# A hybrid attention layer on one core: the first value weights loaded before the second tile of x and rounded on another engine, and one of four partial products left out of the value product

## The chip, the cores and the metric

The kernel runs on one core of a Trainium2 chip. The metric is the time of one execution in microseconds (us); the median of three runs is given. The engines are named as in the profile: PE is TensorE's matmuls, PEld its weight loads, DVE is VectorE, ACT ScalarE, POOL GpSimd, and SP is SyncE, which issues all loads and stores of this kernel in one queue. Names like L365 are line numbers of the kernel before; behind line 494 the changed file's numbers are one lower.

## The reference

One layer on x of 1024 rows by 1024 columns, in float32. Only the first part is touched by the change:

```python
h = rmsnorm(x, norm_mix_g)
z = h @ w_in        # [qA|kA|vA|qB|kB|vB|gA|gB]
# differential attention: 4 heads, two score maps a head, values of width 128
sc = einsum('bqhcd,bkhcd->bchqk', rope(qA), rope(kA)) * 64 ** -0.5
sc = where(k_chunk <= q_chunk, sc, -1e30)      # chunks of 64 rows
p = softmax(sc)
attn = p[:, 0] - lam * p[:, 1]
o = einsum('bhqk,bkhd->bqhd', attn, vA)        # the value product
yA = rmsnorm(o, subln_g) * (1 - lam_init)
# then: band attention yB (8 heads), gated merge, cross attention to 256
# memory rows, a SwiGLU block of inner width 2816, final rmsnorm
```

## The kernel before

**Two parts for each number.** Every float32 operand of a large product is split in two numbers of TensorE's faster fp32r type: `hi`, the operand rounded, and `lo`, the remainder `src - hi` (`split`, L72 to L79). The rounding is a copy on ScalarE (L74) or an operation on GpSimd (L78), as the argument `hi_eng` says; the remainder is taken on VectorE (L79). A product of two split operands then takes three matmuls into one bank, hi by hi, lo by hi and hi by lo (`prod`, L89, and `prod_steps`, L212).

**The value product is built otherwise.** For a block of 128 queries and a block of 128 keys, the transposed probabilities `pt` (hi and lo) are the stationary operands, and the moving one is 256 columns of `v`: 128 columns of v's hi beside 128 columns of v's lo. L364 multiplies pt's hi and L365 pt's lo with all 256, into the bank `av`; that makes four products, hi and lo of `pt` with hi and lo of `v`. At the end of a block the two halves of the bank are added (L369 and L370). A head has 8 query blocks with 1 to 8 key blocks, 36 pairs, and each pair has one L364 and one L365.

**Weights.** `unit` (L81) issues the load of 128 x 1024 weights into `raw` (2 buffers) and splits it into `wsp` (3 buffers). `Units` holds the weights of one job; `Feed` is the list of projection jobs, which the attention code steps through between its own matmuls, so that TensorE has projections (L215 to L217, bank `acc`, two of these) to do while the softmax runs on other engines. `v_jobs(g, ..)` makes the 8 jobs that project one group of values, with two weight units a group; group 0 is the first work of the feed.

**The start.** The loop at L489 goes over 8 tiles of x of 128 rows: load the tile, (for the first) load the gain, then `norm_T`: mean square on ScalarE (L106), reciprocal root on GpSimd (L99, L101), scaling on VectorE (L108), and 8 transposes on TensorE (L120), four into the bank `tr` and four into the bank `av`. Each bank is split by ScalarE (L74) and VectorE (L79) into the stationary tiles `t`. There is one `tr` bank and one `av` bank, so a tile's transposes wait until the banks of the tile before are split. Behind the second tile the first value weights are loaded, and then the value projections follow the tiles at a distance of one.

**The differential attention.** A `UnitA` is one head and one block of 128 queries. `s` makes the scores in a bank `s` (L310, L311; two of these), VectorE takes the maximum (L333), ScalarE the exponentials (L334), and VectorE the difference of the two maps (L340). `tr` transposes up to four key blocks of the result into the one bank `tr` (L350) and splits it into `pt`; `avs` is the value product; `end`, two steps later, transposes the finished block, again in the bank `tr` (L382), and ScalarE copies it out into `yt` (L383). The next transposes of probabilities (L350) can't begin before that copy has emptied the bank.

**The order of the instructions** on each engine is not that of the code: a scheduler reorders the program when it is built, and each engine then works through its row in order.

Of the kernel before, what the change touches and what calls it, by code (L numbers as in the profile page):

```python
# [15 lines left out]
P = 128  # L16
# [19 lines left out]
def build(tc, x, mem, wqk, wv, wg, wup, wout, wcq, wck, wcv, wco, wgu, wdn,  # L36
          bias, lamv, subln_g, g_mix, g_cross, g_mem, g_ffn, g_final, rope, out):
    nc = tc.nc
    pe, act, dve, pool, sp = nc.tensor, nc.scalar, nc.vector, nc.gpsimd, nc.sync
# [17 lines left out]
    def acc_tile():  # L57
        return psum.tile([P, HALF], F32, name="acc", tag="acc", bufs=2)
# [7 lines left out]
    def av_tile():  # L66
        return psum.tile([P, HALF], F32, name="av", tag="av", bufs=1)
# [4 lines left out]
    def split(hi, lo, src, hi_eng, lo_eng):  # L72
        if hi_eng is act:
            act.copy(out=hi, in_=src)  # L74
        elif hi_eng is dve:
            dve.tensor_copy(out=hi, in_=src)
        else:
            pool.tensor_scalar(out=hi, in0=src, scalar1=1.0, scalar2=0.0, op0=ALU.mult, op1=ALU.add)  # L78
        lo_eng.tensor_tensor(out=lo, in0=src, in1=hi.bitcast(F32), op=ALU.subtract)  # L79

    def unit(src, hi_eng=act):  # L81

        raw = wp.tile([P, D], F32, name="raw", tag="raw", bufs=2)
        sp.dma_start(out=raw, in_=src)
        w = wp.tile([P, 2, D], F32R, name="wsp", tag="wsp", bufs=3)
        split(w[:, 0], w[:, 1], raw, hi_eng, dve)
        return w
# [9 lines left out]
    def rstd_of(ss, n):  # L97
        ms = sm.tile([P, 1], F32, name="ms")
        pool.tensor_scalar(out=ms, in0=ss, scalar1=1.0 / n, scalar2=EPS, op0=ALU.mult, op1=ALU.add)  # L99
        r = sm.tile([P, 1], F32, name="rstd")  # L100
        pool.tensor_tensor(out=r, in0=ms, in1=mhalf, op=ALU.pow)  # L101
        return r

    def rms(xt, gbc, dst):
        ss = sm.tile([P, 1], F32, name="ss")
        act.activation(dst, xt, AF.Square, accum_out=ss)  # L106
        r = rstd_of(ss, D)
        dve.scalar_tensor_tensor(out=dst, in0=xt, scalar=r, in1=gbc, op0=ALU.mult, op1=ALU.mult)  # L108

    def norm_T(xt, gbc, xn, dst_of):  # L110

        rms(xt, gbc, xn)
        to_T(xn, dst_of)

    def to_T(xn, dst_of):
        for g in range(2):
            ps = (tr_tile if g == 0 else av_tile)()
            for i in range(4):
                k = g * 4 + i
                pe.transpose(out=ps[:, i * P:(i + 1) * P], in_=xn[:, k * P:(k + 1) * P], identity=ident)  # L120
            hi, lo = dst_of(g)
            v = ps.rearrange("p (a b) -> p a b", a=4)
            split(hi, lo, v, act, dve)
# [88 lines left out]
    def prod_steps(acc, terms, us):  # L212
        n = len(terms)
        for i, (lh, ll, rh, rl) in enumerate(terms):
            pe.matmul(acc, lh, rh, start=(i == 0), stop=False)  # L215
            pe.matmul(acc, ll, rh, start=False, stop=False)  # L216
            pe.matmul(acc, lh, rl, start=False, stop=(i == n - 1))  # L217
            yield us
# [9 lines left out]
    with tc.tile_pool(name="at", bufs=1, reuse_waits="tile") as at:  # L228
        stage[:] = [lambda: at.tile([P, HALF], F32, name="gst", tag="gst", bufs=2)]

        def v_jobs(g, nh, dv):

            ws = Units(wv[2 * g], wv[2 * g + 1], hi_eng=pool if g == 0 else act)
            vt = []

            def run(tt):
                def go(w):
                    if tt % 2 == 0:
                        vt.append(at.tile([P, 2, HALF], F32R, name="v", tag="v", bufs=4))
                    acc = acc_tile()  # L240
                    terms = [(*hT.sta(k, tt), w[k // 4][:, 0, (k % 4) * 256:(k % 4 + 1) * 256],
                              w[k // 4][:, 1, (k % 4) * 256:(k % 4 + 1) * 256]) for k in range(KT)]
                    yield from prod_steps(acc[:, :256], terms, 0.33)
                    dst = vt[tt // 2][:, tt % 2].rearrange("p (h s d) -> p s h d", s=2, d=dv)
                    split(dst[:, 0], dst[:, 1], acc[:, :256].rearrange("p (h d) -> p h d", d=dv), act, dve)
                return go

            return [Job(ws, run(tt)) for tt in range(NT)], lambda kt: vt[kt // 2][:, kt % 2]
# [65 lines left out]
        class UnitA:  # L314
# [40 lines left out]
            def avs(self, k0, pt):  # L355
                b, rs = self.b, self.rs
                hv = (self.h % 2) * 256
                if k0 == 0:
                    self.av = av_tile()
                av = self.av  # L360
                for kt in range(k0, min(k0 + 4, b + 1)):
                    i = kt - k0
                    vk = self.v(kt)[:, hv:hv + 256]
                    pe.matmul(av[:, :256], pt[:, 0, i * P:(i + 1) * P], vk, start=(kt == 0), stop=False)  # L364
                    pe.matmul(av[:, :256], pt[:, 1, i * P:(i + 1) * P], vk, start=False, stop=(kt == b))  # L365
                if k0 + 4 <= b:
                    return
                o = self.o = at.tile([P, 2, P], F32, name="o", tag="o", bufs=3)
                act.copy(out=o[:, 0], in_=av[:, P:2 * P])  # L369
                dve.tensor_tensor(out=o[:, 1], in0=av[:, 0:P], in1=o[:, 0], op=ALU.add)  # L370
                ss = sm.tile([P, 1], F32, name="ssa")
                act.activation(o[:, 0], o[:, 1], AF.Square, scale=rs[:, 0:1], accum_out=ss)
                r = rstd_of(ss, P)
                pool.tensor_tensor(out=r, in0=r, in1=rs[:, 0:1], op=ALU.mult)
                dve.scalar_tensor_tensor(out=o[:, 0], in0=o[:, 1], scalar=r, in1=g08, op0=ALU.mult, op1=ALU.mult)
# [91 lines left out]

        qks = [QK(h, 4 + h, True) for h in range(4)] + [QK(8 + i, 12 + i, False) for i in range(4)]
        vjs = [v_jobs(0, 2, 128), v_jobs(1, 2, 128), v_jobs(2, 4, 64), v_jobs(3, 4, 64)]
        heads = []  # L470
        for i in range(8):
# [11 lines left out]
        for g in gate_order:  # L483
            ws = Units(wg[g])
# [4 lines left out]
        for tt in range(NT):  # L489
            xt = at.tile([P, 2, D], F32, name="xt", tag=("pa", "qst")[tt % 2], bufs=(2, 3)[tt % 2])  # L490
            sp.dma_start(out=xt[:, 0], in_=x[tt * P:(tt + 1) * P, :])
            if tt == 0:
                sp.dma_start(out=gbc, in_=g_mix.partition_broadcast(P))
            norm_T(xt[:, 0], gbc, xt[:, 1], hT.dst(tt))
            if tt == 1:
                vjs[0][0][0].load()
            feed.add(vjs[0][0][tt])
            if tt >= LAG:
                feed.need(vjs[0][0][tt - LAG])
# [41 lines left out]
        for n, (hi, u) in enumerate(flat):  # L541
# [10 lines left out]
            for i, g in enumerate(gs):  # L552
# [4 lines left out]
                pt = u.tr(g)  # L557
# [9 lines left out]
    with tc.tile_pool(name="late", bufs=1, reuse_waits="tile") as lt:  # L567
# [116 lines left out]
        for kh in range(2):  # L684
            for cc in range(2):
                ws = [unit(wout[cc * 4 + kh * 2 + i]) for i in range(2)]
# [537 lines left out]
```

## Time and profile before

| | |
|---|---|
| median of 3 runs | 1808.42 us (1808.24 to 1808.46) |
| span of the profiled execution | 1808.5 us |
| the profiled execution's own time | 1810.3 us |
| PE busy | 1746.3 us (97%) |
| PEld busy | 1472.0 us (81%) |
| DVE busy | 1102.1 us (61%) |
| ACT busy | 765.9 us (42%) |
| POOL busy | 524.5 us (29%) |

The span is the time from the first to the last instruction of one execution that the hardware profiler recorded; the busy times are shares of it. All times in the rows below are of that execution, counted from the start of its span. The granted clock is the share of TensorE's full clock that the chip allowed it; 1.00 is full speed.

### The profile page before, as it was taken

What the parts mean: (1) busy time and instruction counts of PE and PEld (TensorE: products, weight loads), DVE (VectorE), ACT (ScalarE), POOL (GpSimd) and SP (SyncE); (2) the same over time, 40 slices, a digit from 0 to 9 for tenths busy, and PEclk for the clock granted to TensorE, in tenths of its full rate; (3) what the DMA queues carried; (4) which work ended last, traced back from release to release, by engine and by line L of the source; (5) the groups of instructions that cost most, each with busy time, mean ns of one, the idle gap of its engine ahead of it and who ended that gap; (6) DMA issues with size and microseconds to landing.
All of it is one profiled execution on the core that took longest, in us unless ns stands there. A gap on an engine that the chain in (4) does not pass through costs nothing.

```text
span 1808.5 us, 23594 instructions
## 1 busy us (share of the span) xinstructions
PE 1746.3 (97%) x8836; PEld 1472.0 (81%) x8836; DVE 1102.1 (61%) x1491; ACT 765.9 (42%) x1425; POOL 524.5 (29%) x559
## 2 busy tenths in 40 slices
PE   7999999999999999999999999789999999999996
PEld 7778797898898888888888887578888888888885
DVE  6585667646756644445644546886676656655555
ACT  5354455535545544213542244443333333334343
POOL 3232213213323202200000001676666655400001
PEclk9999999999999999999999999989999999999999
DMA  5332313212222265422421123244445435586663
GB/s 191 105 88 68 103 42 102 70 53 62 78 72 68 82 233 196 151 78 71 140 82 59 47 70 140 93 151 182 180 159 190 163 140 186 205 285 195 191 194 117
DMA packets 75731, 229.81 MB, mean 127 GB/s; under 512 B 9184, under 2 KB 9440, under 8 KB 71776
## 3 DMA queue, kind: packets, MB, share of 16 engines
q1 hardware_dynamic: 75616, 228.30, 37.3%
q8 instruction: 69, 1.13, 0.3%
q14 instruction: 46, 0.38, 0.1%
HBM read 160.10 MB, written 55.57 MB: 119 GB/s over the span
## 4 chain that ended last, share of the span: by engine, by line
PE 66%; DVE 3%; issue 2%; ACT 2%; POOL 1%; DMA 0%; DVEq 0%; POOLq 0%; ACTq 0%
PE bk L888 11%; PE bk L889 11%; PE bk L887 11%; PE acc L215 5%; PE acc L216 5%; PE acc L217 5%; PE s L93 2%; PE s L94 2%; PE s L95 2%; PE s L215 2%; PE s L216 2%; PE s L217 2%; PE av L452 1%; DVE T L882 1%; PE tr L436 1%
## 5 line engine op out<-in xcount | busy, mean ns | idle before, releaser
L215 PE MATMUL acc<-t,wsp 128*128 128x512 f32 (+1 forms) x704 | 270.6, 384 | 0.0
L217 PE MATMUL acc<-t,wsp 128*128 128x512 f32 (+1 forms) x704 | 270.5, 384 | 0.0
L216 PE MATMUL acc<-t,wsp 128*128 128x512 f32 (+1 forms) x704 | 270.4, 384 | 0.0
L888 PE MATMUL bk<-T,w 128*128 128x512 f32 x616 | 241.3, 392 | 14.0 <-DVE w L882 14.0
L887 PE MATMUL bk<-T,w 128*128 128x512 f32 x616 | 241.0, 391 | 0.0
L889 PE MATMUL bk<-T,w 128*128 128x512 f32 x616 | 240.6, 391 | 0.0
L882 DVE TENSOR_TENSOR w<-fr,w 128x512 fp32r<-128x512 f32 x132 | 148.3, 1157 | 70.1 <-ACT w L881 69.8
L79 DVE TENSOR_TENSOR wsp<-raw,wsp 128x1024 fp32r<-128x1024 f32 x100 | 124.6, 1246 | 72.2 <-ACT wsp L74 71.0
L74 ACT CAST wsp<-raw 128x1024 fp32r<-128x1024 f32 x98 | 102.7, 1048 | 126.3 <-PE s L217 50.2
L217 PEld LDWEIGHTS acc<-t,wsp 128*128 128x128 f32 x704 | 133.3, 189 | 25.3
L216 PEld LDWEIGHTS acc<-t,wsp 128*128 128x128 f32 x704 | 133.3, 189 | 23.0 <-DVE wsp L79 0.7
L215 PEld LDWEIGHTS acc<-t,wsp 128*128 128x128 f32 x704 | 133.3, 189 | 22.2
L888 PEld LDWEIGHTS bk<-T,w 128*128 128x128 f32 x616 | 116.5, 189 | 39.5 <-DVE w L882 15.3
L882 DVE TENSOR_TENSOR do<-dr,do 128x1024 fp32r<-128x1024 f32 x77 | 96.8, 1260 | 82.8 <-ACT do L881 82.1
L889 PEld LDWEIGHTS bk<-T,w 128*128 128x128 f32 x616 | 116.5, 189 | 24.2
L887 PEld LDWEIGHTS bk<-T,w 128*128 128x128 f32 x616 | 116.3, 189 | 24.4 <-ACT hq L792 0.2
L881 ACT CAST do<-dr 128x1024 fp32r<-128x1024 f32 x77 | 80.9, 1050 | 118.2 <-PE bk L889 102.9
L215 PE MATMUL acc<-wsp,t 128*128 128x256 f32 (+1 forms) x384 | 124.7, 325 | 1.0 <-POOL wsp L78 1.0
L217 PE MATMUL acc<-wsp,t 128*128 128x256 f32 (+1 forms) x384 | 122.9, 320 | 1.5 <-DVE wsp L79 1.5
L216 PE MATMUL acc<-wsp,t 128*128 128x256 f32 (+1 forms) x384 | 123.0, 321 | 0.0
L888 PE MATMUL bk<-do 128*128 128x512 f32 x308 | 120.2, 390 | 1.3 <-DVE do L882 1.3
L889 PE MATMUL bk<-do 128*128 128x512 f32 x308 | 119.8, 389 | 0.0
(204 smaller groups left out, 3726.2 us busy)
## 6 DMA issues: line engine op xcount, KB each, us to landing
fr<-in_wgu SPq DMA_DIRECT2D x44, 512.0 KB, 5.2
dw<-in_wdn SPq DMA_DIRECT2D x22, 512.0 KB, 5.2
wd<-dw SPq DMA_DIRECT2D x11, 1024.0 KB, 3.9
ad<-r SPq DMA_DIRECT2D x22, 512.0 KB, 3.4
sd<-s SPq DMA_DIRECT2D x11, 1024.0 KB, 4.2
dr<-sd SPq DMA_DIRECT2D x44, 256.0 KB, 3.8
dr<-wd SPq DMA_DIRECT2D x44, 256.0 KB, 4.0
dr<-ad SPq DMA_DIRECT2D x33, 256.0 KB, 5.0
```

The source lines that it names most:

```text
L74: act.copy(out=hi, in_=src)
L79: lo_eng.tensor_tensor(out=lo, in0=src, in1=hi.bitcast(F32), op=ALU.subtract)
L93: pe.matmul(acc, lh, rh, start=(i == 0), stop=False)
L94: pe.matmul(acc, ll, rh, start=False, stop=False)
L215: pe.matmul(acc, lh, rh, start=(i == 0), stop=False)
L216: pe.matmul(acc, ll, rh, start=False, stop=False)
L217: pe.matmul(acc, lh, rl, start=False, stop=(i == n - 1))
L881: self.act.copy(out=hi, in_=src)
L882: self.dve.tensor_tensor(out=lo, in0=src, in1=hi.bitcast(F32), op=ALU.subtract)
L887: mm(acc, l[0], r[0], start=start, stop=False, skip_group_check=onto)
L888: mm(acc, l[1], r[0], start=False, stop=False, skip_group_check=onto)
L889: mm(acc, l[0], r[1], start=False, stop=stop, skip_group_check=onto)
```

## The change

Three edits. The first value weights are rounded on ScalarE, no longer on GpSimd (L233). The second matmul of the value product of the differential attention has 128 moving columns, v's hi, no longer 256: the product of the two lo parts is left out (L365). The two loads of the first value weights, with the splits behind them, stand ahead of the second tile of x, no longer behind its norm and transposes (L495).

```diff
@@ v_jobs
-            ws = Units(wv[2 * g], wv[2 * g + 1], hi_eng=pool if g == 0 else act)
+            ws = Units(wv[2 * g], wv[2 * g + 1], hi_eng=act)
@@ UnitA.avs
                     vk = self.v(kt)[:, hv:hv + 256]
                     pe.matmul(av[:, :256], pt[:, 0, i * P:(i + 1) * P], vk, start=(kt == 0), stop=False)
-                    pe.matmul(av[:, :256], pt[:, 1, i * P:(i + 1) * P], vk, start=False, stop=(kt == b))
+                    pe.matmul(av[:, :P], pt[:, 1, i * P:(i + 1) * P], vk[:, :P], start=False, stop=(kt == b))
@@ the loop over the tiles of x
             if tt == 0:
                 sp.dma_start(out=gbc, in_=g_mix.partition_broadcast(P))
+                vjs[0][0][0].load()
             norm_T(xt[:, 0], gbc, xt[:, 1], hT.dst(tt))
-            if tt == 1:
-                vjs[0][0][0].load()
             feed.add(vjs[0][0][tt])
```

The edits also change the order that the scheduler makes. In SP's queue the two loads of weights now stand behind the gain and ahead of tile 1 of x. On ScalarE at the start, before (`xt` is a tile of x, `wsp` a split weight unit, `tr` and `av` the banks with the transposes):

```order
L106 ACTIVATE xt,ss<-xt 128x1024 x2
L74 CAST t_107<-tr 128x4x128
L74 CAST t_109<-av 128x4x128
L106 ACTIVATE xt,ss<-xt 128x1024
L74 CAST t_107<-tr 128x4x128
```

and with the change:

```order
L106 ACTIVATE xt,ss<-xt 128x1024
L74 CAST wsp<-raw 128x1024 x2
L106 ACTIVATE xt,ss<-xt 128x1024
L74 CAST t_107<-tr 128x4x128
L106 ACTIVATE xt,ss<-xt 128x1024
L74 CAST t_109<-av 128x4x128
```

The two casts of weights are new on this engine and stand between the mean squares of tile 0 and tile 1. On VectorE at the start, before:

```order
L108 SCALAR_TENSOR_TENSOR xt<-xt,rstd,gbc 128x1024 x2
L79 TENSOR_TENSOR wsp<-raw,wsp 128x1024
L79 TENSOR_TENSOR t_108<-tr,t_107 128x4x128
L79 TENSOR_TENSOR t_110<-av,t_109 128x4x128
L79 TENSOR_TENSOR wsp<-raw,wsp 128x1024
```

and with the change:

```order
L108 SCALAR_TENSOR_TENSOR xt<-xt,rstd,gbc 128x1024
L79 TENSOR_TENSOR wsp<-raw,wsp 128x1024 x2
L108 SCALAR_TENSOR_TENSOR xt<-xt,rstd,gbc 128x1024
L79 TENSOR_TENSOR t_108<-tr,t_107 128x4x128
L108 SCALAR_TENSOR_TENSOR xt<-xt,rstd,gbc 128x1024
L79 TENSOR_TENSOR t_110<-av,t_109 128x4x128
```

Both remainders of weights now come ahead of the scaling of tile 1, and the scaling of tile 2 comes between the two remainders of tile 0. In the first head, on TensorE, where the block of six key blocks has its scores behind it and the block ahead of it is transposed (`tr<-ident,pp`), before:

```order
L365 MATMUL av<-v,pt 128x256
L364 MATMUL av<-v,pt 128x256
L350 MATMUL tr<-ident,pp 128x128 x4
L365 MATMUL av<-v,pt 128x256
L364 MATMUL av<-v,pt 128x256
L365 MATMUL av<-v,pt 128x256
L215 MATMUL acc<-t_111,wsp 128x512
```

and with the change:

```order
L365 MATMUL av<-v,pt 128x128
L364 MATMUL av<-v,pt 128x256
L365 MATMUL av<-v,pt 128x128
L215 MATMUL acc<-t_111,wsp 128x512
L216 MATMUL acc<-t_111,wsp 128x512
L217 MATMUL acc<-t_112,wsp 128x512
L350 MATMUL tr<-ident,pp 128x128 x4
```

The transposes now stand behind the last value matmuls and three projections. On ScalarE at the same place, before (`qst` is the split queries, `r` the projection read for the rotation, `yt` the copy that empties the bank `tr`):

```order
L293 CAST qst<-rf 64x512
L294 CAST qst<-rf 64x512
L372 ACTIVATE o,ssa<-o,rs 128x128
L284 ACTIVATE r_1079<-acc 128x512
L334 ACTIVATE pp,sums<-s,nmx 128x768
L383 COPY yt<-tr 128x128
L74 CAST wsp<-raw 128x1024
L334 ACTIVATE pp,sums<-s,nmx 128x768
```

and with the change:

```order
L372 ACTIVATE o,ssa<-o,rs 128x128
L293 CAST qst<-rf 64x512
L294 CAST qst<-rf 64x512
L284 ACTIVATE r_1079<-acc 128x512
L74 CAST wsp<-raw 128x1024
L334 ACTIVATE pp,sums<-s,nmx 128x768 x2
L383 COPY yt<-tr 128x128
```

The cast of a weight unit and both exponentials now stand ahead of the copy into `yt`.

## Rows read from the trace of the kernel before

**Rows 1.** Stretches: length; PE, PEld, DVE, ACT, POOL busy; clock, DMA share, GB/s.

```profile
0.00:15.00 15.00, 3.11 (x12) 2.42 (x13) 6.53 (x6) 5.90 (x9) 6.80 (x15) 1.00 0.85 315
15.00:45.00 30.00, 30.00 (x245) 30.00 (x244) 21.84 (x34) 17.43 (x34) 6.80 (x11) 1.00 0.36 130
45.00:380.00 335.00, 324.26 (x1746) 274.71 (x1745) 217.14 (x427) 167.71 (x411) 85.93 (x134) 0.99 0.27 83
```

**Rows 2.** Timeline of the start: start us, us, engine, line, operation, idle before.

```profile
6.44 1.28 DVE L108 SCALAR_TENSOR_TENSOR xt<-xt,rstd,gbc 128x1024 f32<-128x1024 f32 x1 [6.44 <-DMA gbc<-in_g_mix]
...
7.65 1.06 ACT L106 ACTIVATE xt<-xt 128x1024 f32<-128x1024 f32 x1 [2.40 <-DMA xt<-in_x]
...
9.69 3.02 POOL L78 TENSOR_SCALAR wsp<-raw 128x1024 fp32r<-128x1024 f32 x2
9.75 2.06 DVE L108 SCALAR_TENSOR_TENSOR xt<-xt,rstd,gbc 128x1024 f32<-128x1024 f32 x1 [2.03 <-POOL rstd L101]
...
11.49 1.06 ACT L106 ACTIVATE xt<-xt 128x1024 f32<-128x1024 f32 x1 [1.12 <-DMA xt<-in_x]
11.73 2.05 DVE L79 TENSOR_TENSOR wsp<-raw,wsp 128x1024 fp32r<-128x1024 f32 x1
...
13.70 0.68 DVE L79 TENSOR_TENSOR t<-tr,t 128x512 fp32r<-128x512 f32 x1
...
14.44 1.12 PE L120 MATMUL tr<-ident,xt 128*128 128x128 f32 x4 [3.06 <-DVE t L79]
14.90 1.21 DVE L79 TENSOR_TENSOR wsp<-raw,wsp 128x1024 fp32r<-128x1024 f32 x1
```

**Rows 3.** TensorE's waits, 45 to 380 us: us in total, times, longest.

```profile
PE tr L350 <- ACT yt L383: 5.0, 8, 1.7
```

**Rows 4.** Timeline of the first head, 103.4 to 107.2 us.

```profile
104.24 0.89 ACT L334 ACTIVATE pp<-s,nmx 128x768 f32<-128x768 f32 x1
...
105.12 0.26 ACT L383 COPY yt<-tr 128x128 f32<-128x128 f32 x1
105.26 1.06 ACT L74 CAST wsp<-raw 128x1024 fp32r<-128x1024 f32 x1
...
105.43 0.66 PE L350 MATMUL tr<-ident,pp 128*128 128x128 f32 x4 [1.13 <-ACT yt L383]
...
105.84 0.36 PE L365 MATMUL av<-v,pt 128*128 128x256 f32 x1
...
106.28 0.40 PE L215 MATMUL acc<-t,wsp 128*128 128x512 f32 x1
...
106.85 0.90 ACT L334 ACTIVATE pp<-s,nmx 128x768 f32<-128x768 f32 x1 [0.53 <-DVE nmx L333]
106.97 0.39 PE L215 MATMUL acc<-t,wsp 128*128 128x512 f32 x1
```

**Rows 5.** Timeline of TensorE, 136.7 to 138.4 us.

```profile
136.82 0.28 PE L365 MATMUL av<-v,pt 128*128 128x256 f32 x1
...
137.53 0.28 PE L365 MATMUL av<-v,pt 128*128 128x256 f32 x1
137.65 0.22 PE L310 MATMUL s<-kst,qst 128*128 128x128 f32 x1
...
138.05 0.44 PE L215 MATMUL acc<-t,wsp 128*128 128x512 f32 x1
```

**Rows 6.** Timeline of TensorE, 75 to 80 us.

```profile
75.20 0.39 PE L310 MATMUL s<-kst,qst 128*128 128x256 f32 x1 [2.00 <-ACT pp L334]
```

**Rows 7.** A stretch, columns as in rows 1.

```profile
70.00:80.00 10.00, 8.00 (x32) 6.04 (x31) 7.42 (x18) 4.03 (x10) 5.49 (x4) 0.83 0.44 151
```

**Rows 8.** Timeline of the first head, 109.4 to 110.8 us.

```profile
109.47 0.39 PE L217 MATMUL acc<-t,wsp 128*128 128x512 f32 x1
...
110.75 0.60 ACT L284 ACTIVATE r<-acc 128x512 f32<-128x512 f32 x1
```

**Rows 9.** Timeline of TensorE, 119 to 121 us.

```profile
119.86 0.66 PE L350 MATMUL tr<-ident,pp 128*128 128x128 f32 x4 [1.73 <-ACT yt L383]
```

## The prediction

> **What bounds the kernel now.** I read the busy times by stretch first [rows 1]. They split the program's front into three. In the first 15 us TensorE works for 3.11 us: it waits for the first tiles of x. From 15 to 45 us it has no gap at all, so whatever lets that run begin earlier or later moves everything behind it. From 45 to 380 us, where the differential attention runs, it is busy for 324.26 of 335 us; the 10.7 us that are left are waits. So TensorE is the bound, and the change can touch the time in three ways: by the moment at which the steady run begins, by the pace of the value product, and by those waits.
>
> Next I read the start in order of time [rows 2]. The chain that lets TensorE begin at 14.44 us is on VectorE. Tile 1 of x is on the chip at 7.65 us, its mean square is taken, and VectorE scales it from 9.75 us on. That takes 2.06 us and the first weight remainder behind it 2.05 us, since GpSimd rounds the same weights next to them from 9.69 us on; alone they take 1.28 us (the row at 6.44) and 1.21 us (the row at 14.90). Only then comes the remainder of tile 0's first half (13.70 us, 0.68 us), which frees the bank that tile 1's transposes want.
>
> Last I read who waits in the attention [rows 3]: eight times, 5.0 us in all, the transposes of the probabilities wait for ScalarE's copy into yt, which empties their bank.
>
> **The start: -0.2 us.** The queue of loads now runs x tile 0, gain, two weight units, x tile 1, x tile 2. Before, the third load landed by 7.65 us and the sixth by 11.49 us [rows 2], so one load takes (11.49 - 7.65) / 3 = 1.28 us, and tile 1, now fifth, lands at 7.65 + 2 x 1.28 = 10.21 us. The weights are there at 7.65 and 8.93 us. ScalarE rounds each in 1.06 us (price of the same cast in [rows 4]), done at 8.71 and 9.99 us, so it is free when tile 1 lands. VectorE takes both remainders at 1.21 us each, done by 11.2 us. From the start of the square to the start of the scaling took 9.75 - 7.65 = 2.10 us, so the scaling starts at 12.31 us, lasts 1.28 us, and the remainder of tile 0 behind it starts 0.08 us before that ends, as it did before: 13.51 + 0.68 + 0.06 = 14.25 us for TensorE instead of 14.44. What the rounding gives back (0.8 us twice) the late tile eats. What is queued behind the new casts on ScalarE is the square of tile 1 and then tile 0's own casts, which end near 12.0 us, before VectorE wants them. Rounding on ScalarE costs nothing here because its row is empty until 10.21 us; without that cover it would be 2 x 1.06 us. Both ends: -0.5 us if tile 1 lands a little sooner, +1.1 us if everything comes one load later. The rope table also moves ahead of the last two tiles of x; those are used long after they land.
>
> **The narrow matmuls: -0.8 us.** 4 heads x 36 pairs = 144 matmuls go from 256 to 128 moving columns. In a row of 256-column matmuls the starts go from 136.82 to 137.53 us in six steps, 0.118 us each [rows 5]. Right behind stand four matmuls of 128 columns of the same type. The last 256-column one ends at 137.81 us, the 512-column one behind the four at 138.49 us: 0.68 us for five. A 512-column one takes (106.97 - 106.28) / 3 = 0.23 us [rows 4], so the four cost 0.45 us, 0.112 us each. Half the columns saves 0.006 us, not half: 144 x 0.006 = 0.8 us. Ends: nothing, and half of the pace, 144 x 0.059 = 8.5 us. A loss is excluded: no 128-column row is slower. I take the row of the same shape and type.
>
> The Trainium skill, page "TensorE: Matmul & The Clock Gate", section "Back-to-back issue gap", has the gap go with the columns, about 56 ns at 128 and 109 ns at 256; by that the edit would give an estimated 7.7 us. The same page's section "LDWEIGHTS (loading the stationary operand)" has 107 ns for loading 128 columns of weights, whatever moves; by that it would give next to nothing. The trace agrees with the second, at 0.112 us.
>
> **The order in the attention: +2.3 us.** The scheduler draws up the rows anew, and they differ in many small places; the largest that I can cost is in the first head. Before, ScalarE copied into yt behind the first exponential of the six-block unit: copy at 105.12, and TensorE's transposes at 105.43 us, after a wait of 1.13 us [rows 4]. In the new row the cast of a weight unit and both exponentials stand ahead of that copy. The cast (1.06 us) only moves the first exponential to 105.30 us. The second one did not start before 106.85 us, since it waited for a maximum from VectorE. The copy starts 0.88 us after an exponential does (104.24 to 105.12) and takes 0.26 us, so it ends at 107.99 us, and TensorE goes on at 108.04 us. TensorE has more to do first: three value matmuls (105.84 to 106.28, 0.44 us) and three projections (0.69 us). It was free at 105.43 - 1.13 = 104.30 us, so it stands still from 105.43 to 108.04 us: 2.6 us instead of 1.1, late by 1.5 us.
>
> A wait of that length has a second price. After the wait of 2.00 us that ended at 75.20 us [rows 6] TensorE's clock fell to 1.2 GHz: the granted share from 70 to 80 us is 0.83 [rows 7], which is 0.17 x 10 = 1.7 us of work lost. 2.6 us is more than 2.00, so I add 1.7 us. Some of the 3.2 us is swallowed at the next link: the projection that ends at 109.47 + 0.39 = 109.86 us is not read by ScalarE before 110.75 us [rows 8], 0.9 us of slack. That leaves 1.5 + 1.7 - 0.9 = +2.3 us. Ends: -1.1 us, where the copy comes in time and the old wait is gone, and +2.6 us, where nothing is swallowed and the wait is not cut by the three projections. The other shifts, some earlier and some later, I take as nothing in sum; they are why the range is not narrower.
>
> **Sum.** -0.2 - 0.8 + 2.3 = +1.3 us. The profiled execution had a span of 1808.5 us and 1810.3 us by its own clock; the runs without a profile have a median of 1808.42 us. Differences of the span carry over one to one: 1809.7 us. The stretch behind 380 us keeps its order but for a few instructions and is only shifted.
>
> **Rivals.**
> 1. The narrow matmuls give back what their columns say. Speaks for it: half the data. Against: the four 128-column rows. It gives 1809.7 - (8.5 - 0.8) = 1802.0 us. The first of the skill's two rules above is this case. Chance 0.05.
> 2. The copy is not late. If VectorE's new row has the second maximum ready early, the exponentials run back to back, the three projections cover the copy, and the old wait of 1.1 us goes: 1808.4 - 0.2 - 0.8 - 1.1 = 1806.3 us. For it: the scheduler put the transposes later. Against: the maximum waits for the same projection's rotation as before. Chance 0.18, and 0.08 of it goes below 1804.8 us if other waits shrink too.
> 3. Slower: a second long wait in the same head, at the next unit. The transposes at 119.86 us waited 1.73 us for the copy [rows 9], with no fall of the clock behind it. VectorE's new row has a weight remainder (1.21 us) ahead of the maxima there, and two projections (0.46 us) more stand ahead of the transposes: 1.73 + 1.21 - 0.46 = 2.5 us. It decides where that passes 2.0 us: then the clock falls once more, and 0.7 + 1.7 = 2.4 us come on top: 1812.1 us. Against: the units behind a late TensorE find ScalarE further ahead. Chance 0.21.
> 4. The early load does not do what it says: tile 1, and so the steady run, comes one load time late, +1.1 instead of -0.2 us: 1811.0 us. For it: two units of weights stand ahead of the tile that TensorE waits for. Chance 0.10.
>
> **How the numbers follow.** My forecast has 0.46, with a range of its own from 1808 to 1811.5 us. What a measurement of this kernel can tell from no change is about 0.2%, so 1804.8 and 1812.0 us. Below lie rival 1 and part of 2: 0.13. Above lie most of rival 3 (0.18) and the tail of 4 (0.02): 0.20. The rest, 0.67, is no change that counts. The range from 1805.0 to 1813.5 us leaves out rival 1, the low tail of 2 and the high tail of 3.
>
> **What would show it.** TensorE's steady run starts at 14.0 to 14.5 us; tile 1's square starts near 10.2 us; VectorE's scaling of it takes 1.3 instead of 2.06 us. The 128-column value matmuls go at 0.11 us. The transposes near 108 us wait 2.6 us for ScalarE's copy, and projections at 0.43 us stand behind them. I am wrong if the steady run starts after 15 us, if those matmuls go at 0.06 us, or if that wait is under 1.5 us.

## The result and the profile after

The changed kernel takes 1820.51 us (median of 6 runs, 1819.69 to 1821.41) against 1808.44 us (median of 6 runs, 1807.36 to 1809.58): ratio 1.0066, interval 1.0056 to 1.0077. It is slower by about 12 us; the forecast was 1809.7 us. The profiled execution has a span of 1818.2 us, 9.7 us more than the one of before. That one took 1.9 us longer than the median of its kernel, this one (1819.98 us) 0.5 us less than its median; 9.7 + 1.9 + 0.5 = 12.1 us is the difference of the medians, so the two traces show 9.7 us of the loss; the rest is how far each of the two executions lies from its median.

The stretches of the kernel after, with the columns of [rows 1]:

```profile
0.00:15.00 15.00, 2.92 (x11) 2.23 (x12) 5.94 (x6) 8.71 (x13) 3.59 (x14) 1.00 0.88 317
15.00:45.00 30.00, 29.66 (x240) 29.27 (x239) 20.91 (x33) 15.72 (x32) 7.15 (x11) 1.00 0.36 129
45.00:380.00 335.00, 317.11 (x1695) 267.86 (x1693) 212.84 (x418) 165.32 (x402) 83.29 (x130) 0.98 0.27 80
```

The start hardly moved. From 45 to 380 us TensorE is busy for 317.11 us where it was 324.26: 7.2 us more of waiting in the same stretch. The view that answers to [rows 3], TensorE's waits from 45 to 380 us (in total, times, longest), says who made it wait:

```profile
PE tr L350 <- ACT yt L383: 14.0, 14, 3.1
PE s L310 <- ACT pp L334: 2.0, 1, 2.0
```

The transposes of the probabilities wait for the copy into yt 14 times in place of 8, for 14.0 us in place of 5.0. The timeline of the first head, where [rows 4] stand for before:

```profile
104.38 0.33 PE L364 MATMUL av<-v,pt 128*128 128x256 f32 x1
104.55 0.22 PE L365 MATMUL av<-v,pt 128*128 128x128 f32 x1
104.61 0.34 PE L364 MATMUL av<-v,pt 128*128 128x256 f32 x1
104.74 1.05 ACT L74 CAST wsp<-raw 128x1024 fp32r<-128x1024 f32 x1
...
106.31 0.90 ACT L334 ACTIVATE pp<-s,nmx 128x768 f32<-128x768 f32 x1 [0.52 <-DVE nmx L333]
...
107.90 0.90 ACT L334 ACTIVATE pp<-s,nmx 128x768 f32<-128x768 f32 x1 [0.60 <-DVE nmx L333]
...
108.79 0.26 ACT L383 COPY yt<-tr 128x128 f32<-128x128 f32 x1
...
109.10 0.66 PE L350 MATMUL tr<-ident,pp 128*128 128x128 f32 x4 [3.12 <-ACT yt L383]
```

ScalarE works through its row: cast, exponential, exponential, and only then the copy. It starts 4.4 us after the transpose whose bank it empties has ended (at 104.4 us); both exponentials wait for VectorE's maxima, too. TensorE stands still for 3.12 us. The granted clock, in stretches of the kernel before and then of the one after (columns as in [rows 1]):

```profile
105.00:115.00 10.00, 9.31 (x49) 7.93 (x50) 7.56 (x14) 5.33 (x15) 2.68 (x6) 1.00 0.59 158
185.00:195.00 10.00, 9.32 (x49) 7.50 (x48) 9.35 (x16) 5.94 (x13) 4.82 (x5) 1.00 0.41 131
300.00:313.00 13.00, 11.01 (x47) 8.42 (x46) 10.80 (x24) 6.01 (x17) 4.09 (x8) 0.87 0.56 181
```

```profile
105.00:115.00 10.00, 6.67 (x28) 5.02 (x26) 7.79 (x12) 4.86 (x13) 2.56 (x5) 0.83 0.51 132
185.00:195.00 10.00, 7.88 (x38) 6.39 (x36) 7.87 (x12) 5.29 (x13) 2.83 (x6) 0.83 0.47 131
300.00:313.00 13.00, 12.67 (x70) 10.66 (x71) 9.57 (x19) 5.46 (x14) 4.92 (x6) 1.00 0.50 144
```

After, the clock is at 1.2 GHz for a part of two of these stretches (0.83 over 10 us, twice), before in one (0.87 over 13 us): 2 x 0.17 x 10 - 0.13 x 13 = 1.7 us more work lost. The fall of [rows 7], 0.83 from 70 to 80 us, is in both traces.

The start: the second four transposes of the sixth tile of x before, and then the timeline of the kernel after, from the first weights to the same transposes:

```profile
31.47 0.60 PE L120 MATMUL av<-ident,xt 128*128 128x128 f32 x4
```

```profile
9.07 2.52 DVE L79 TENSOR_TENSOR wsp<-raw,wsp 128x1024 fp32r<-128x1024 f32 x2 [1.17 <-ACT wsp L74]
...
10.58 1.06 ACT L106 ACTIVATE xt<-xt 128x1024 f32<-128x1024 f32 x1 [0.25 <-DMA xt<-in_x]
...
12.69 1.28 DVE L108 SCALAR_TENSOR_TENSOR xt<-xt,rstd,gbc 128x1024 f32<-128x1024 f32 x1 [1.10 <-POOL rstd L101]
...
14.63 1.11 PE L120 MATMUL tr<-ident,xt 128*128 128x128 f32 x4 [1.79 <-DVE t L79]
...
29.35 1.28 DVE L108 SCALAR_TENSOR_TENSOR xt<-xt,rstd,gbc 128x1024 f32<-128x1024 f32 x1 [0.72 <-POOL rstd L101]
...
30.89 0.68 DVE L79 TENSOR_TENSOR t<-tr,t 128x512 fp32r<-128x512 f32 x1
...
31.62 0.66 PE L120 MATMUL tr<-ident,xt 128*128 128x128 f32 x4 [0.34 <-DVE t L79]
32.22 0.66 PE L120 MATMUL av<-ident,xt 128*128 128x128 f32 x4
```

TensorE begins its second tile at 14.63 us, where it was 14.44, and by 32 us it is 0.75 us late. All of TensorE's waits from 45 to 460 us (the rows of 0.3 us and more of the view of waits) went from 11.8 to 18.4 us. So of the 9.7 us the sum has: waits 6.6, clock 1.7, start 0.8, together 9.1 us. The 0.6 us that are left, in which smaller gains and losses cancel, are not assigned.

### The profile page after: what moved, and what is told of

Read it like the earlier page. It is cut to its first block, busy times and chain, and to the rows that moved or that the text cites. A ratio compares the mean times of both kernels' runs of the same rounds, so it can differ in the third digit from the quotient of the medians.

```text
span 1818.2 us, 23599 instructions
## 1 busy us (share of the span) xinstructions
PE 1749.3 (96%) x8836; PEld 1474.0 (81%) x8836; DVE 1102.1 (61%) x1491; ACT 769.0 (42%) x1427; POOL 521.1 (29%) x557
## 4 chain that ended last, share of the span: by engine, by line
PE 66%; DVE 3%; issue 2%; ACT 1%; POOL 1%; DMA 0%; DVEq 0%; POOLq 0%; ACTq 0%
PE bk L887 11%; PE bk L888 11%; PE bk L886 11%; PE acc L215 5%; PE acc L216 5%; PE acc L217 5%; PE s L94 2%; PE s L95 2%; PE s L93 2%; PE s L217 2%; PE s L215 2%; PE s L216 2%; PE av L452 1%; DVE T L881 1%; PE tr L436 1%
```

## The experiments

**Content and order apart.** The edits can be undone one by one, and the order can be held. For the second, the program is built twice: the row of each engine is read from the first build, and in the second each instruction gets an edge to the one ahead of it in that row, an edge of order alone, without a wait. `program(n, rows)` builds the kernel before with n columns in the second value matmul, and with its rows pinned to `rows` where these are given; with n = 128 the product of the two lo parts is left out. The edits below that name `program` are written against it, and the kernel before is `program(256)`.

```python
def pin(tc, rows):
    ins = {i.name: i for i in tc.nc.cur_bb.bb.instructions}
    for names in rows.values():
        names = [n for n in names if n in ins]
        for a, b in zip(names, names[1:]):
            tc.add_manual_dep(ins[b], a, mybir.DependencyInfo(mybir.DependencyClass.NoSync,
                              mybir.DependencyReason.DATA), reason="row order")
```

The rows show that the edits of the start change the order in the start alone, and that all the new order of the attention comes with the narrow matmul. So four kernels. The start alone:

```diff
-            ws = Units(wv[2 * g], wv[2 * g + 1], hi_eng=pool if g == 0 else act)
+            ws = Units(wv[2 * g], wv[2 * g + 1], hi_eng=act)
...
                 sp.dma_start(out=gbc, in_=g_mix.partition_broadcast(P))
+                vjs[0][0][0].load()
             norm_T(xt[:, 0], gbc, xt[:, 1], hT.dst(tt))
-            if tt == 1:
-                vjs[0][0][0].load()
```

> The kernel before with the two edits of the start alone (early load, rounding on ScalarE); all value matmuls keep 256 columns, and the order of the attention is that of before. Theory A (the new order in the attention makes the kernel slower): the start is worth what the trace of after shows at 39 us, +0.8 us, so a ratio of 1.0004, within 0.1%. Rival B (the narrow matmuls themselves are slow): the same. Rival C (the start is late and the attention meets its weights in another phase): about the whole difference, +10 to +12 us, 1.006.

Measured: 1811.44 us, ratio 1.0012 (1.0003 to 1.0021), a loss of 0.5 to 3.8 us. The narrow matmul alone:

```diff
-                    pe.matmul(av[:, :256], pt[:, 1, i * P:(i + 1) * P], vk, start=False, stop=(kt == b))
+                    pe.matmul(av[:, :P], pt[:, 1, i * P:(i + 1) * P], vk[:, :P], start=False, stop=(kt == b))
```

> The kernel before with the narrow value matmul alone (the product of the two lo parts is left out); the start is that of before, and the order of the attention is that of after. Theories A and B: +10 to +12 us, ratio 1.006. Rival C: under 1 us, 1.000.

Measured: 1822.11 us, 1.0072 (1.0059 to 1.0085). The same matmul, with the rows held to those of the build with 256 columns:

```diff
-    nc = program(256)
+    nc = program(128, rows_of(program(256)))
```

> The value matmul with 128 columns (the product of the two lo parts is left out), but every engine keeps the row of instructions of the kernel before; the start is that of before. Theory A: the matmuls alone are worth -0.8 us (144 x 0.006 us), so 1808 us or a little less, ratio 0.9995 and no sum of waits for the copy above that of before, 5.0 us. Rival B: +10 us, 1.006. A third answer, the columns give back what they say (144 x 0.059 us): -8.5 us, 0.995.

Measured: 1809.39 us, 1.0002 (0.9993 to 1.0011). And the mirror of it:

```diff
-    nc = program(256)
+    nc = program(256, rows_of(program(128)))
```

> All value matmuls with 256 columns as before, but every engine has the row of instructions that the scheduler makes for the narrow ones; the start is that of before. Theory A: the whole loss of the attention and no gain of the matmuls, +11 to +13 us, ratio 1.0065, with about 14 us of waits of the transposes for the copy. Rivals B and C: no difference to before, within 1 us.

Measured: 1822.00 us, 1.0071 (1.0059 to 1.0084). The waits of the transposes, 45 to 460 us, in the run with old rows and then in the run with 256 columns and new rows:

```profile
PE tr L350 <- ACT yt L383: 5.5, 9, 1.8
```

```profile
PE tr L350 <- ACT yt L383: 14.5, 13, 2.8
```

In the attention the order is the whole loss, with either width; the width alone changes nothing that can be measured. Rivals B and C are out, and so are the 8.5 us that half the columns would give. In both pinned runs the rows of ScalarE, VectorE and GpSimd in the trace are those of the build that they were read from, but for single records.

**Is it the copies?** In the rows made for the narrow matmul (128 columns, the product of the two lo parts left out), ScalarE's row alone is edited (`COPIES` has the names of the 32 copies into yt, counted from 0):

```diff
+def up(rows, moves):              # copy number: places up
+    act = next(r for r in rows.values() if COPIES[0] in r)
+    for k, n in moves.items():
+        i = act.index(COPIES[k])
+        act.insert(i - n, act.pop(i))
+    return rows
...
+    nc = program(128, up(rows_of(program(128)), {1: 3, 2: 1, 3: 1, 8: 1, 9: 2, 11: 2, 13: 1, 17: 1,
+                                                 18: 1, 20: 2, 21: 1, 22: 4, 25: 1, 26: 2, 29: 1, 30: 1}))
```

> The narrow value matmul with the rows that the scheduler makes for it (as in the run of the narrow matmul alone), but on ScalarE 16 of the 32 copies into yt are moved up by one to four places, to where their transposes have ended; every other row is kept. Theory A (the loss is the place of the copies): the waits of the transposes for the copy fall from 14.1 us to under 4 us, the second fall of the clock goes, and the time returns to 1807 to 1811 us, ratio 1.000. Rival D (the loss lies in the rest of the new rows; the copies only show it): the waits go over to the exponentials or the maxima, and the time stays above 1817 us, 1.005.

Measured: 1815.91 us, 1.0038 (1.0026 to 1.0051). Half of the loss is gone, half stays: between theory A and rival D. Its waits, 45 to 460 us:

```profile
PE tr L350 <- ACT yt L383: 4.9, 4, 1.8
PE s L310 <- ACT pp L334: 3.8, 3, 2.0
PE tr L382 <- DVE pt L79: 3.3, 2, 3.1
PE s L310 <- POOL qst L295: 2.8, 1, 2.8
```

The waits for the copy fell from 14.1 to 4.9 us (under 4 were expected), but the next user of the same bank, the transpose L382, now waits for VectorE's remainder of pt, and the scores for the split queries. One copy alone, the one of the forecast:

```diff
+    nc = program(128, up(rows_of(program(128)), {1: 3}))
```

> As the run with the narrow matmul alone, but one single copy of the 32 moved: the one at 108.59 us goes ahead of the weight cast and the two exponentials. Theory A with the prices of the prediction: the wait of 2.8 us goes and with it the fall of the clock, 1.7 us, so -3 to -4.5 us against 1822.1 us: about 1818 us, and a granted clock of 1.00 from 105 to 115 us. If the clock costs nothing there: -1.5 us, the growth of the wait alone. Rival D: no change, 1822 us.

Measured: 1820.11 us, 1.0060 (1.0047 to 1.0073): 2 us less than the run with the narrow matmul alone, with intervals that overlap, so that no change (rival D) isn't excluded, and less than the 3 to 4.5 us expected. Its timeline shows why:

```profile
106.43 0.91 ACT L334 ACTIVATE pp<-s,nmx 128x768 f32<-128x768 f32 x1 [0.60 <-DVE nmx L333]
...
108.62 0.56 ACT L74 CAST pt<-tr 128x512 fp32r<-128x512 f32 x1
...
110.37 0.69 DVE L79 TENSOR_TENSOR pt<-tr,pt 128x512 fp32r<-128x512 f32 x1
...
111.11 0.33 PE L382 MATMUL tr<-ident,o 128*128 128x128 f32 x1 [3.10 <-DVE pt L79]
```

The transposes of the probabilities begin at 104.66 us without a wait, but the split that empties the bank behind them stands in both rows behind the same exponentials: the rounding starts at 108.62, the remainder at 110.37 us. TensorE waits for 3.10 us at the next transpose. The wait wasn't removed but handed on.

The same in the rows of before, with 256 columns and six copies (numbers 1, 3, 9, 11, 25 and 26) up by one or two places:

> The kernel before, with 256 columns and its own rows, but six copies into yt moved up by one or two places on ScalarE. Theory A: the six waits together are 1.13 + 1.73 + 0.53 + 0.68 + 0.15 + 0.15 = 4.4 us; so -4 us, 1804 to 1805 us, ratio 0.998. Rival D: nothing, 1809 us.

Measured: 1807.79 us, 0.9993 (0.9984 to 1.0002): 1.3 us faster, with an interval from a gain of 2.9 to a loss of 0.4 us, where 4 us were expected. Of the waits for the copy 1.8 us are left, but 2.1 and 1.1 us of waits for pt have come in their place. The scheduler's own way, on the changed kernel:

```diff
-                act.copy(out=yt[:, self.b * P:(self.b + 1) * P], in_=tr[:, :P])
+                with tc.high_priority():
+                    act.copy(out=yt[:, self.b * P:(self.b + 1) * P], in_=tr[:, :P])
```

> The changed kernel (all three edits) with the copy into yt marked as preferred for the scheduler, which then makes new rows by itself: in the first head the copy stands between the two exponentials again, in many other places it stands where it was, and other instructions move too. Theory A: what the moved copies save, 2 to 6 us against 1820.5 us, so 1814 to 1818 us, if the other moves cost nothing. Rival D: 1820 us, or any other number, since the rows are new.

Measured: 1819.14 us, 1.0053 (1.0040 to 1.0067). The waits for the copy are 14.0 us, as in the changed kernel (14.1 us over the same stretch): the mark doesn't help.

**Whose row?** The rows of ScalarE and VectorE depend on each other and were only exchanged together, with those of GpSimd and of the loads; TensorE's row is set against those of the other four, in the narrow kernel. `mix` takes the rows of the engines that it names from the old build, the others from the new.

```diff
+    nc = program(128, mix(rows_of(program(128)), rows_of(program(256)), ['PE']))
```

> The narrow value matmul; TensorE alone keeps the row of the kernel before, the other engines have the rows that the scheduler makes for the narrow matmul. Theory A2 (the loss is in the rows of ScalarE and VectorE, where the steps that empty the bank tr, the copy into yt and both halves of the split of pt, stand behind exponentials and weights): the whole loss stays, 1820 us or more, since TensorE now comes to the bank even sooner. Rival E (the loss is TensorE's own row, which puts its transposes at other places among the projections): back near before, 1808 to 1811 us. If neither row alone makes it but their mismatch does, this run and the next are both slow.

Measured: 1821.37 us, 1.0071 (1.0059 to 1.0084). And the other four from the old build:

```diff
+    nc = program(128, mix(rows_of(program(128)), rows_of(program(256)), ['Activation', 'DVE', 'Pool', 'SP']))
```

> The mirror of the run with TensorE's old row: the narrow value matmul, TensorE has the new row, the other four engines keep the rows of the kernel before. Theory A2: no loss, 1806 to 1811 us, and less than 6 us of waits for the copy. Rival E: the whole loss, about 1822 us. Mismatch: slow as well, over 1815 us.

Measured: 1813.11 us, 1.0025 (1.0016 to 1.0034). The new rows of the other four engines cost the whole loss even with TensorE's old row; TensorE's new row alone costs 4.5 us, which none of the three expectations has. The two don't add up (12.8 and 4.5 us against 13.0 us together), and ScalarE's row wasn't told from VectorE's. Then every step that empties the bank, moved up in the new rows:

```diff
+    nc = program(128, up(rows_of(program(128)), (COPIES, {1: 3, 2: 1, 3: 1, 8: 1, 9: 2, 11: 2, 13: 1, 17: 1,
+                                                          18: 1, 20: 2, 21: 1, 22: 4, 25: 1, 26: 2, 29: 1, 30: 1}),
+                         (CASTS, {4: 3, 6: 2, 16: 1, 17: 2, 18: 2, 32: 2, 36: 1, 40: 1, 41: 1}),
+                         (RESTS, {4: 6, 6: 2, 16: 3, 17: 2, 18: 2, 40: 2, 41: 2})))
```

> As the run with 16 copies moved up, and beside them nine roundings of pt on ScalarE and seven remainders of pt on VectorE moved up in their rows, to where the transposes of the probabilities have ended: every step that empties the bank tr and was late in that run's trace. Theory A2: the waits at 112.3 (3.1 us) and 126.9 us (1.0 us) go, most of the fall of the clock too, so -4 to -6 us against 1815.9 us: 1810 to 1812 us. Rival D (there is always a next thing that is late): above 1814.5 us.

Measured: 1812.65 us, 1.0028 (1.0018 to 1.0037). This is just above the 1810 to 1812 us of theory A2. From 1.0072 by 1.0038 to 1.0028: the steps that empty `tr` account for about 8 of the 13 us of the narrow kernel (5 to 11 us, by the two intervals). What is left has another place. The first two lines and the stretch are of this run (two extra lines in this file move the copy to L384), the last line is of the kernel before:

```profile
PE tr L350 <- ACT yt L384: 5.5, 5, 1.6
PE s L310 <- POOL qst L295: 3.3, 1, 3.3
185.00:195.00 10.00, 8.55 (x36) 6.99 (x35) 8.08 (x12) 3.58 (x8) 5.53 (x6) 0.83 0.42 138
```

```profile
PE s L310 <- POOL qst L295: 0.9, 1, 0.9
```

The waits for the bank are back at those of before, the scores wait 3.3 us for the split queries where it was 0.9 in before, and from 185 to 195 us the clock falls, where before it had 1.00.

**Are these rows a bad draw, or any new rows?** The kernel before, 256 columns, with one constant of the feed changed, so that the work stays and the rows are drawn anew:

```diff
-F0, FA, FB, W0, W1 = 3, 5.5, 3.8, 0.3, 1.2
+F0, FA, FB, W0, W1 = 3, 5.4, 3.8, 0.3, 1.2
```

> The kernel before with 256 columns, and one constant of its feed changed by 2%: 5.4 in place of 5.5 us of projections put between the steps of a unit of the first four heads. The work is the same; the scheduler makes new rows, about as many differences as the narrow matmul makes. Theory F (the rows of before are a good draw, and new rows cost whatever made them): +3 us or more, 1812 to 1822 us. Rival G (the rows made for the narrow matmul are a bad draw): within 2 us of before.

Measured: 1820.06 us, 1.0066 (1.0052 to 1.0079): the same loss as the changed kernel's, without any of its edits. Its waits:

```profile
PE tr L350 <- ACT yt L383: 10.0, 9, 2.8
PE tr L350 <- DVE pt L79: 3.6, 3, 1.9
```

With 5.6 and 256 columns:

> The kernel before with 256 columns and 5.6 in place of 5.5 us of projections put between the steps of a unit; the rows differ from those of before from the fourth part of the attention on only (a tenth as many differences on TensorE as with 5.4). Theory F (the rows of before are a good draw): slower by 2 to 12 us, less than with 5.4, since less is new. Rival G: within 2 us of before.

Measured: 1813.36 us, 1.0026 (1.0017 to 1.0034). With 5.4 and 128 columns:

> The narrow value matmul with 5.4 in place of 5.5 us of projections put between the steps of a unit; new rows again. Theory F: +4 to +13 us, like the other new rows. Rival G: a better draw than that of 5.5, within 3 us of before.

Measured: 1824.88 us, 1.0087 (1.0074 to 1.0100). With 5.6 and 128 columns:

> The narrow value matmul with 5.6 us; the rows of the first half are those of the narrow matmul with 5.5. Theory F: about +12 us, as with 5.5, since the waits of the first half stay. Rival G: within 3 us of before.

Measured: 1828.89 us, 1.0108 (1.0095 to 1.0121), the slowest, with the most waits of all for the copy:

```profile
PE tr L350 <- ACT yt L383: 19.3, 16, 3.5
```

Five sets of rows that the scheduler drew, for two widths and three constants, cost 4.7 to 19.5 us more than those of before. Theory F holds and rival G falls, though two of the losses are larger than F expected (15.7 and 19.5 us): the rows for the narrow matmul are not an odd draw; those of before are a good one. Two limits: the five are not independent (with 5.6 the rows are the known ones up to about 200 us), and the constant also changes how many projections stand between the steps. No run held the rows while the constant changed, so it isn't shown that the row order alone makes these four losses. Last, the old rows with the bank emptied sooner:

```diff
+    nc = program(128, up(rows_of(program(256)), (COPIES, {1: 2, 3: 1, 4: 1, 9: 1, 11: 1, 25: 2, 26: 2, 27: 1}),
+                         (CASTS, {4: 1, 6: 1, 16: 2, 18: 2}), (RESTS, {4: 3, 6: 6, 16: 1, 18: 2})))
```

> The narrow value matmul with the rows of the kernel before, in which eight copies into yt, four roundings of pt on ScalarE and four remainders of pt on VectorE are moved up to where the transposes have ended. Theory A2 (what holds the bank tr is what costs): the waits for the copy and for the remainder of pt fall from 6 us to under 3 us: 1804 to 1806.5 us, ratio 0.998. Rival D (there is always a next thing that is late): 1808 to 1809 us, as in the run with the old rows alone.

Measured: 1807.45 us, 0.9990 (0.9981 to 0.9999), the lowest median here, and 0.2 to 3.4 us faster than before. The median lies between the two expectations: the waits fell to 2.3 us as theory A2 has it, the time by less. Its wait for the copy:

```profile
PE tr L350 <- ACT yt L384: 2.3, 5, 1.0
```

**All runs together.** The last column is the sum of the waits of L350 and L382 for the copy or for pt, 45 to 460 us, in one profiled execution each.

| kernel | ratio to before | waits for the bank, us |
|---|---|---|
| before | 1 | 5.3 |
| old rows, bank emptied sooner, 128 | 0.9990 | 2.3 |
| old rows, copies up, 256 | 0.9993 | 5.0 |
| old rows, 128 | 1.0002 | 5.8 |
| start alone | 1.0012 | 5.2 |
| TensorE's row new, the others old, 128 | 1.0025 | 7.7 |
| constant 5.6, 256 | 1.0026 | 9.7 |
| new rows, bank emptied sooner, 128 | 1.0028 | 5.5 |
| new rows, copies up, 128 | 1.0038 | 9.2 |
| copy preferred | 1.0053 | 14.0 |
| new rows, one copy up, 128 | 1.0060 | 14.6 |
| constant 5.4, 256 | 1.0066 | 14.5 |
| the changed kernel | 1.0066 | 14.4 |
| new rows, 256 | 1.0071 | 14.8 |
| TensorE's row old, the others new, 128 | 1.0071 | 15.2 |
| narrow alone | 1.0072 | 14.4 |
| constant 5.4, 128 | 1.0087 | 16.1 |
| constant 5.6, 128 | 1.0108 | 19.6 |

The two columns go together. A microsecond more of these waits costs more than one: 14.3 us more of them go with 1.08%, which is 19.5 us, and 9.1 us with 11.9 us, about 1.3 each. The clock after long waits may be the rest; that wasn't taken apart. Where edited rows moved the wait elsewhere (new rows, bank emptied sooner) the time is above what the column says.

## Why the prediction was wrong

**The bound** was read rightly: TensorE, and in the attention its waits; the loss came in there.

**The step that failed** is the last sentence of the part on the order: "The other shifts, some earlier and some later, I take as nothing in sum". The one place that was walked through came out much as forecast: the copy stands behind both exponentials, the transposes wait 3.12 us against the 2.6 forecast, and the clock falls. But 14 places wait for the copy, not one, and one of the others for 2.0 us. The new order by itself, with 256 columns, costs 12.8 us (1.0071), where the sum had 2.3: if the 2.3 stand, the term for the other places, set to zero, is about +10 us. Moving 16 copies up in the new rows takes back half of the loss. Counting late copies would not have been enough to see it coming: by the traces 12 of the 32 copies stand behind an exponential, a cast or another copy that began after their transpose had ended, and in the kernel before it is 9 of 32. What differs is how long TensorE then waits, and that takes the whole walk at each place. Nor did the range cover it, since it was made from the ends of one place. Its upper end there is too low by its own terms, too: 1.5 + 1.7 us with nothing swallowed, and 0.7 us of projections that don't cut the wait, are 3.9 us and not 2.6.

**The reason given for zero**, that shifts go both ways, takes old and new rows for two draws of the same kind. The five other draws say that they aren't: all were slower. Why before's rows are good was not tested; that its rows and constants were themselves kept for their time is a guess that no run here shows.

**The price of a wait.** The wait that the copy made was taken as the bank's whole story. In the run with one copy moved, the bank was held next by the split of pt, for 3.10 us: any gain or loss in a bank with one buffer has to be followed to its next user.

**The narrow matmul** fits: -0.8 us forecast, -1.3 to +2.0 us measured with the old rows, an interval that also holds zero. In the trace after, a pair of 256 and 128 columns goes in 0.23 us (L364 at 104.38 and again at 104.61 us), where two of 256 took 2 x 0.118 us. Each has weights of its own to load. The Trainium skill, page "TensorE: Matmul & The Clock Gate", section "LDWEIGHTS (loading the stationary operand)", gives 128 / 1.2 = 107 ns for a load of 128 columns, an estimated 0.21 us for two; the trace agrees, at 0.23 us. By the formula in the same page's section "Back-to-back issue gap", N / 2.4 + 2.5 ns, the pair would take an estimated 0.165 us, which is not what this trace shows. That section calls it the gap of an isolated matmul and says that in a stream with a weight load for each matmul both set the pace; the prediction left that out.

**The start** was forecast at -0.2 us and is +0.8 us in the trace. The first links came as forecast or late by 0.4 us (square at 10.58 us, scaling 1.28 us with no GpSimd beside it, TensorE at 14.63 instead of 14.25). What the forecast left out is VectorE's row behind that: the scalings of the last tiles (the last at 29.35 us, which waits 0.72 us for GpSimd's root) stand ahead of the remainder at 30.89 us that frees the bank `tr`, and TensorE waits for it until 31.62 us.

One trace can't give the start to better than a microsecond, though. TensorE takes 0.21 us for each of the first value projections and 0.12 us later, with a granted clock of 1.00 throughout; in the traces of before and after the quicker pace begins at about 18.1 us, in the run with the start alone at 20.4 us. Two pairs of starts, the first of the kernel after, the second of the run with the start alone, and that run's transposes:

```profile
19.17 0.28 PE L215 MATMUL acc<-wsp,t 128*128 128x256 f32 x1
19.29 0.28 PE L216 MATMUL acc<-wsp,t 128*128 128x256 f32 x1
```

```profile
19.13 0.41 PE L217 MATMUL acc<-wsp,t 128*128 128x256 f32 x1
19.34 0.41 PE L215 MATMUL acc<-wsp,t 128*128 128x256 f32 x1
...
33.25 0.66 PE L120 MATMUL av<-ident,xt 128*128 128x128 f32 x4
```

So that run's execution is 1.8 us late at the same transposes (31.47 us before). In the 15 traces with the start of before they begin at 31.02 to 32.57 us, in the three with the new start at 32.22, 32.24 and 33.25 us. The run with the start alone has a loss of 0.5 to 3.8 us; the new start costs something, and how much stays open within that.

**The rivals.** The second long wait (rival 3) was placed at the next unit and priced 2.5 us; the trace after has 0.9 us there (at 123.55 us), and the next long one came in the second head. That the clock falls where a wait passes 2.0 us, on which its price rests, does not hold in these traces (last section). Rival 2, the copy in time, fell with the 3.12 us.

**What stays open** is the rest of the loss once the bank is emptied in time, 5.1 us (1.0028). The trace of that run shows 2.4 us of it as a longer wait for the split queries and about 1.7 us as one fall of the clock more; no run took either away.

## What to carry to other kernels

Where a scheduler draws up the rows, an edit has two prices, its own and that of the new order: hold the order with edges and measure each alone before judging the edit. A kernel that was measured with one set of rows can lose more by a new draw (0.26 to 1.08% in the five draws here) than an edit of this size can win (0.8 us forecast, 0.04%). And when one buffer is shared by several users, walk through all steps that empty it, at every use: repairing one hands the wait to the next.

## What the hardware showed unexpectedly

The fall of TensorE's clock is not decided by the length of the wait ahead of it. In the kernel before, the wait of 2.00 us that ended at 75.20 us [rows 6] is followed by a fall [rows 7]. In the run with 128 columns and the old rows the same wait, behind the same rows, isn't (2.04 us):

```profile
76.10 0.39 PE L310 MATMUL s<-kst,qst 128*128 128x256 f32 x1 [2.04 <-ACT pp L334]
70.00:80.00 10.00, 7.09 (x34) 5.35 (x32) 7.61 (x15) 3.16 (x9) 4.62 (x3) 1.00 0.52 172
```

Nor is it in the run with the start alone, and neither is the wait of 1.60 us near 308 us, which in before has 0.87 around it:

```profile
76.96 0.39 PE L310 MATMUL s<-kst,qst 128*128 128x256 f32 x1 [2.00 <-ACT pp L334]
```

```profile
70.00:80.00 10.00, 7.99 (x38) 6.00 (x36) 6.83 (x12) 3.20 (x8) 4.62 (x3) 1.00 0.58 194
300.00:313.00 13.00, 10.94 (x58) 8.56 (x57) 10.81 (x20) 5.89 (x16) 5.26 (x9) 1.00 0.56 171
```

All 18 traces have the wait near 75 us, at 1.99 to 2.05 us. In 11 of them the granted clock from 70 to 82 us is 0.86, in six it is 1.00, and one has about 0.95 through its whole execution. So the 1.7 us of a fall come and go between executions, and one trace is sure to no better than that. What decides it is open.
